# Small products of different tilings placed behind each other, and the scan's state given its own turn on VectorE and TensorE

## The chip, the cores and the metric

The kernel runs on one core of a Trainium2 chip. The metric is device time in microseconds (us) of one launch. A difference is given against the kernel before, measured on the same chip.

## The reference

One layer of a streaming encoder, sequence 256, width 4096, in fp32. A combined projection feeds 16 heads of forgetting attention (fox) and 32 heads of an RWKV-7 scan; both are gated, projected back, added to the residual and normalised.

```python
proj = jnp.einsum('bsd,dc->bsc', x, w_in)
# fox: softmax(q k^T / sqrt(128) + cumulated log forget gates) v, causal, 16 heads of 128
# rwkv: token shift, decay w, in-context rate a, normalised key kk, then per head of 64:
def frame_step(state, inp):
    r_t, w_t, k_t, v_t, a_t, b_t = inp
    sa = jnp.einsum('bhvk,bhk->bhv', state, a_t)
    state = (state * w_t[:, :, None, :] + sa[..., None] * b_t[:, :, None, :]
             + v_t[..., None] * k_t[:, :, None, :])
    return state, jnp.einsum('bhvk,bhk->bhv', state, r_t)
# group norm of y, a bonus term, then
h = jnp.concatenate([fox_out, rwkv_out], axis=-1) * jax.nn.silu(z)
x = layernorm(ALPHA * x + jnp.einsum('bsc,cd->bsd', h, w_out)) * ln_gain + ln_bias
```

## The kernel before, in words

**Large products.** Every fp32 operand of the two big projections is split into a high and a low half of a reduced format; `hi*hi`, `lo*hi` and `hi*lo` are summed in PSUM. The input projection runs over 8 head groups `n` (4 rwkv heads and 2 fox heads each) times 4 blocks `b` of 512 columns; a block takes 16 weight tiles `w{n}_{b}_{q}`, and each tile gives 12 products of 128x512, named `acc`. The output projection does the same with `wo` and `oacc`. A weight tile comes by DMA, ScalarE casts its high half (`w...h`, four buffers), VectorE subtracts for the low half (`w...l`, three buffers).

**Small products.** Between the large ones stand those of the attention and the scan. Of the scan, per head group: `gp` (pairwise products within a chunk, array tiled 64x128), `qt` and `xp` (assembling an inverse of blocks, array tiled 32x32), and then, for each of 4 chunks `c` of 64 frames:

- `rh` (`residual(c)`): state `SV` times the chunk's keys, tiled 128x64; VectorE copies it to `R`;
- `up`: inverse times `R`, on the whole array; ScalarE copies it to `UV`;
- `sp` (not in the last chunk): the state's update from `UV`, tiled 128x64; VectorE copies or adds it into `SV` of the next chunk, one half of the partitions (`j` = 0, 1) at a time; from the second chunk on it adds `sl`, the decayed state, which ScalarE makes;
- `yp`: the chunk's output from `SV` and `UV`, tiled 128x64.

So each chunk's `rh` needs the `SV` that came out of the `sp` before it. A small fp32 product appears as two instructions in the profile.

**What sets the order.** No instruction is issued when the code calls it. `Later` records every operation, and `flush` lays them out with a planner: it simulates the engines with estimated durations (`span_of`), gives each engine's free time to the ready operation with the lowest `key`, and issues in the resulting order. `main` marks the large products. Consecutive small products form one batch (`batches`) and are placed together. `mode_of` names the array's tiling: 0 for the whole array, else the tile's size; the planner charges its constant `SWITCH` (190) for a change of mode and prefers operations of the current mode while it is in a tiled one. `seen` adds the constant margin (`MARGIN`, 1000, for TensorE in the main part) to the end of what an operation waits for. Buffers are counted by `places`. Engines then run their queues in that order, and real waits are by semaphores.

Of the kernel before, what the change touches and what calls it, by code (L numbers as in the profile page):

```python
# [86 lines left out]
AHEAD = 100000  # L87
SWITCH = 190
MARGIN = 1000


MASKS = {}
# [52 lines left out]
def span_of(engine, name, args, out, ins):  # L145

    if engine == "tensor":
        n = columns(out)
        if name == "transpose":
            hold = max(2 * n / 2.4, 112)  # L150
        elif ins[-1].dtype == BF16:
            hold = 427
        elif ins[-1].dtype == F32R:
            hold = max(n * 17 / 16 / 2.4, 113)
        else:
            tile = rounded(int(ins[0].ap[0][1])), rounded(columns(ins[0]))
# [12 lines left out]
    n = max(columns(a) for a in [out, *ins])  # L169
    if engine == "vector":  # L170
        if name == "reciprocal":
            t = 130 + 6.32 * n
        elif name in ("tensor_copy", "tensor_scalar") and not any(is_psum(a) for a in [out, *ins]):
            t = 175 + n / 1.92
        else:
            t = 157 + n / 0.96 + (20 if any(is_psum(a) for a in ins) else 0)
        return max(t - 75, 60), t + 35
    if engine == "scalar":
        t = 195 + n / 1.2 + (0 if name == "copy" else 50)
        if "accum_out" in args:  # L180
# [25 lines left out]


class Op:
    __slots__ = ("engine", "call", "args", "kwargs", "hold", "lag", "after", "touches", "key", "main", "mode", "table", "parts", "bank", "ready", "start", "end")


class Later:


    def __init__(self, tc):
        self.tc, self.ops, self.count = tc, [], 0
        self.free = dict.fromkeys(ENGINES, 0.0)
        self.moved = 0.0
        self.writes, self.reads, self.banks = {}, {}, {}
        self.slots, self.left, self.main = {}, {}, False  # L220
        self.mode, self.table, self.floor, self.early = 0, 0, 0.0, set()
        self.stay = set()
        self.sooner = 0
        for e in ENGINES:
            setattr(self, e, Engine(self, e, getattr(tc.nc, e)))

    def take(self, engine, call, name, args, kwargs):
        op = Op()
        op.engine, op.call, op.args, op.kwargs = engine, call, args, kwargs
        aps = [a for a in args if hasattr(a, "tensor")]  # L230
        outs = [kwargs["out"]] if "out" in kwargs else [aps.pop(0)]
        ins = aps + [a for k, a in kwargs.items() if k not in ("out", "accum_out") and hasattr(a, "tensor")]
        if "accum_out" in kwargs:
            outs.append(kwargs["accum_out"])
        op.hold, op.lag = span_of(engine, name, kwargs, outs[0], ins)
        op.after, op.touches = set(), []
        op.main = self.main
        op.mode = mode_of(engine, name, ins)
        op.table = table_of(args, kwargs) if engine == "scalar" else 0
        op.key = self.count - self.sooner  # L240
        self.count += 1
        op.end = None
        for ap, writing in [(a, False) for a in ins] + [(a, True) for a in outs]:
            t = ap.tensor
            if not hasattr(t, "tag_meta"):
                continue
            where = t.name
            at = extent(ap)
            if where not in self.writes:
                self.writes[where], self.reads[where] = [], []  # L250
                if ap.space != bass.MemoryType.DRAM:
                    tag = t.tag
                    self.slots.setdefault(tag, [[self.floor if '_rp' in tag else 0.0] * (t.tag_meta.bufs or 1), []])[1].append(where)
                    self.left[where] = [tag, 0, 0.0, False]
            if where in self.left:
                self.left[where][1] += 1
                op.touches.append(where)
            for other, box in self.writes[where] + (self.reads[where] if writing else []):
                if box[0] < at[1] and at[0] < box[1] and box[2] & at[2] and other is not op:
                    op.after.add(other)  # L260
            (self.writes if writing else self.reads)[where].append((op, at))
        if engine == "tensor":
            bank = op.bank = outs[0].tensor.name
            if bank in self.banks:
                op.after.add(self.banks[bank])
            self.banks[bank] = op
        self.ops.append(op)

    def flush(self, stay=(), closing=None, margin=0):
# [9 lines left out]
        held = []  # L279

        def admit(op):
            op.ready = max([0.0] + [self.seen(o, op, margin) for o in op.after])
            heapq.heappush(soon[op.engine], (op.ready, op.key, id(op), op))

        for op in ops:
# [9 lines left out]
        while done < len(ops):  # L295
# [18 lines left out]
                heapq.heappush(ready[e], (op.key, id(op), op))  # L314
            _, _, op = heapq.heappop(ready[e])
            if e == "tensor" and self.mode and op.mode != self.mode:
                same = [x for x in ready[e] if x[2].mode == self.mode]
                if same:
                    heapq.heappush(ready[e], (op.key, id(op), op))
                    first = min(same)  # L320
                    ready[e].remove(first)
                    heapq.heapify(ready[e])
                    op = first[2]
            wait = self.places(op)
            if wait is None:
                held.append(op)
# [40 lines left out]
    def batches(self):  # L367

        out, last = [], None
        for op in self.ops:  # L370
            op.parts = [op]
            if op.engine == "tensor":
                if last and not op.main and op.mode == last.mode and (op.mode or op.bank == last.bank):
                    own = {id(o) for o in last.parts}
                    if not any(any(id(b) in own for b in o.after) for o in op.after if o.engine != "tensor"):
                        last.parts.append(op)
                        continue
                last = None
                if not op.main:
                    last = Op()  # L380
                    for a in ("engine", "main", "mode", "table", "key", "call", "bank"):
# [35 lines left out]
    def begin(self, op, at):  # L417
        if op.engine == "tensor" and op.mode != self.mode:
            at += SWITCH
            self.mode = op.mode  # L420
        if op.table and op.table != self.table:
            at += 1283
            self.table = op.table
# [27 lines left out]
def layer(ctx: ExitStack, tc: tile.TileContext, xt, xtok, w_lora, w_main, muv, w_o, up, par, mulora, fbias, lng, lnb, cst, out):  # L451
# [424 lines left out]
    def rwkv(n):  # L876
# [138 lines left out]
        for c in range(NCH):  # L1015
# [439 lines left out]
```

## Time and profile before

| | |
|---|---|
| median of 3 timed runs | 1947.29 us (1946.33 to 1948.76) |
| the profiled execution | 1950.54 us, its span 1948.8 us |
| granted TensorE clock | 0.998 |
| PE (TensorE) busy | 1936.5 us (99%) |
| DVE (VectorE) busy | 1370.1 us (70%) |
| ACT (ScalarE) busy | 988.2 us (51%) |
| DMA queue q1, share of 16 engines | 73.3% |

A row of the timeline gives the start, the duration, the engine, line and operation, output and inputs by the program's names, their shapes and how many were merged into the row; in square brackets stands the idle time of the engine before it and what ended it. All operations are issued from one line of the planner (L361), so groups are told apart by tile names. Numbers of buffers and head groups are left out of names there: `acc` is a large product, `w_4l` the low half of weight tile 4 of some block.

### The profile page before, as it was taken

The numbers are of one execution on the slowest core, as the hardware profiler recorded it, in microseconds if no ns is written. First come the engines' busy times: TensorE is split into PE (matmuls) and PEld (weight loads), VectorE is DVE, ScalarE is ACT, GpSimd is POOL, SyncE is SP. The second block draws the span as 40 slices with busy tenths as digits, with TensorE's granted clock in tenths as the row PEclk, the third lists the DMA queues.
The fourth block names the chain that finished last, engine by engine and source line by source line (L and its number), as shares of the span: only waits on it lengthen the run. The fifth ranks groups of instructions, "written<-read, shape, count | busy, mean of one in ns | idle before, by whom it ended". The sixth has DMA issues, their size and how long they took to land.

```text
span 1948.8 us, 28294 instructions
## 1 busy us (share of the span) xinstructions
PE 1936.5 (99%) x10153; PEld 1588.1 (81%) x10153; DVE 1370.1 (70%) x2212; ACT 988.2 (51%) x1485; POOL 75.3 (4%) x111
## 2 busy tenths in 40 slices
PE   9999999999999999999999999999999999999998
PEld 8888888878887888788878887888788878888886
DVE  6687678856885688578856885788578845765555
ACT  6554465445544654465446544654464544443332
POOL 0010001000100010001000100010001000000000
PEclk9999999999999999999999999999999999999999
DMA  9678767877787778777877787778677866866664
GB/s 335 178 207 235 221 190 199 244 201 205 202 238 201 212 200 240 201 209 200 237 200 207 202 235 200 215 200 239 192 215 207 309 201 205 285 201 199 200 194 162
DMA packets 269393, 420.14 MB, mean 216 GB/s; under 512 B 142338, under 2 KB 171028, under 8 KB 269252
## 3 DMA queue, kind: packets, MB, share of 16 engines
q1 hardware_dynamic: 268820, 417.91, 73.3%
q8 instruction: 80, 1.31, 0.3%
q14 instruction: 61, 0.50, 0.1%
q10 hardware_dynamic: 432, 0.43, 0.1%
HBM read 388.61 MB, written 29.64 MB: 215 GB/s over the span
## 4 chain that ended last, share of the span: by engine, by line
PE 98%; DMA 1%; DVE 0%; ACT 0%; DVEq 0%; issue 0%; SPq 0%
PE acc L361 73%; PE oacc L361 18%; PE accl L361 1%; PE yp L361 1%; PE gp L361 1%; PE up L361 1%; PE rh L361 1%; PE lp L361 1%; PE fsp L361 1%; PE fop L361 1%; PE sp L361 0%; PE np L361 0%; DMA h<-hd 0%; PE bkt L361 0%; PE fpt L361 0%; PE xp L361 0%
## 5 line engine op out<-in xcount | busy, mean ns | idle before, releaser
L361 PE MATMUL acc<-w_3h,x 128*128 128x512 f32 x248 | 80.3, 397 | 0.0
L361 PE MATMUL acc<-w_8h,x 128*128 128x512 f32 x248 | 79.9, 399 | 0.0
L361 PE MATMUL acc<-w_5h,x 128*128 128x512 f32 x248 | 79.7, 398 | 0.0
L361 PE MATMUL acc<-w_9h,x 128*128 128x512 f32 x248 | 79.2, 396 | 0.0
L361 PE MATMUL acc<-w_11h,x 128*128 128x512 f32 x248 | 78.9, 395 | 0.0
L361 PE MATMUL acc<-w_7h,x 128*128 128x512 f32 x248 | 78.8, 398 | 0.0
L361 PE MATMUL acc<-w_2h,x 128*128 128x512 f32 x248 | 78.5, 397 | 0.0
L361 PE MATMUL acc<-w_10h,x 128*128 128x512 f32 x248 | 78.1, 392 | 0.0
L361 PE MATMUL acc<-w_15h,x 128*128 128x512 f32 x248 | 77.9, 395 | 0.0
L361 PE MATMUL acc<-w_12h,x 128*128 128x512 f32 x248 | 77.7, 394 | 0.0
L361 DVE TENSOR_REDUCE xc<-prod 128x8 f32<-128x16 f32 (+30 forms) x248 | 73.0, 295 | 6.2
L361 PE MATMUL acc<-w_4h,x 128*128 128x512 f32 x248 | 77.2, 392 | 0.0
L361 PE MATMUL acc<-w_6h,x 128*128 128x512 f32 x248 | 77.0, 391 | 0.0
L361 PE MATMUL acc<-w_0h,x 128*128 128x512 f32 x248 | 76.7, 391 | 0.0
L361 PE MATMUL acc<-w_1h,x 128*128 128x512 f32 x248 | 76.7, 390 | 0.0
L361 PE MATMUL acc<-w_13h,x 128*128 128x512 f32 x248 | 76.5, 389 | 0.0
L361 PE MATMUL acc<-w_14h,x 128*128 128x512 f32 x248 | 76.4, 389 | 0.0
L361 DVE TENSOR_TENSOR prod<-Nb,xc 128x8 f32<-128x8 f32 (+30 forms) x248 | 71.3, 287 | 4.0 <-DMA Nb<-nd 0.4
L361 ACT CAST w_9h<-w 128x1024 fp32r<-128x1024 f32 x31 | 32.7, 1055 | 61.5 <-PE acc L361 54.4
L361 DVE TENSOR_TENSOR w_6l<-w,w_6h 128x1024 fp32r<-128x1024 f32 x31 | 38.0, 1225 | 35.0 <-PE acc L361 34.3
L361 ACT CAST w_14h<-w 128x1024 fp32r<-128x1024 f32 x31 | 32.6, 1051 | 57.9 <-PE acc L361 34.6
L361 DVE TENSOR_TENSOR w_7l<-w,w_7h 128x1024 fp32r<-128x1024 f32 x31 | 38.2, 1233 | 32.2 <-PE acc L361 16.0
(656 smaller groups left out, 5491.1 us busy)
## 6 DMA issues: line engine op xcount, KB each, us to landing
w<-in_w_main_dram SPq DMA_DIRECT2D x496, 512.0 KB, 3.9
wo<-in_w_o_dram SPq DMA_DIRECT2D x128, 512.0 KB, 3.6
bt<-bk SPq DMA_DIRECT2D x88, 128.0 KB, 4.6
Nb<-nd SPq DMA_DIRECT2D x16, 512.0 KB, 6.9
wr<-in_w_main_dram SPq DMA_DIRECT2D x15, 512.0 KB, 6.9
hd<-hl SPq DMA_DIRECT2D x29, 256.0 KB, 5.0
h<-hd SPq DMA_DIRECT2D x29, 256.0 KB, 5.7
raw<-bt SPq DMA_DIRECT2D x16, 256.0 KB, 6.8
```

Source lines behind the costliest of these rows:

```text
L361: ins = op.call(*op.args, **op.kwargs)
```

## The change

Five things, all in the planner and the scan.

- A batch may now hold products of different tilings behind each other (`batches`), as long as none of them waits for another engine's result that the batch itself feeds. Its readiness is worked out part by part (`admit`).
- Operations can be marked `urgent`: `rh` from the second chunk on, and the writes of `SV`. They get a very low `key`, and `seen` gives them a margin of 40 only.
- TensorE, in a tiled mode, may stand idle up to `PATIENCE` = 300 for an urgent batch of the same mode, and otherwise takes another tiled batch before a whole-array one.
- VectorE does not begin an operation that would still run when an urgent one comes ready.
- `rh` and the writes of `SV` are issued half by half, `j` = 1 first, in the order in which `sp` makes the halves.

```diff
@@ span_of
         elif ins[-1].dtype == BF16:
-            hold = 427
+            hold = 427 * n / 512
@@ Later.take
-        op.key = self.count - self.sooner
+        op.urgent = self.urgent
+        op.key = self.count - self.sooner - 2 * AHEAD * self.urgent
...
+        op.earliest = self.earliest
@@ flush
         def admit(op):
-            op.ready = max([0.0] + [self.seen(o, op, margin) for o in op.after])
+            op.ready, at = op.earliest, 0.0
+            for part in op.parts:
+                op.ready = max([op.ready] + [self.seen(o, op, margin) - at for o in part.after if o not in op.parts])
+                at += part.hold
...
             if e == "tensor" and self.mode and op.mode != self.mode:
-                same = [x for x in ready[e] if x[2].mode == self.mode]
-                if same:
+                soonest = [x for x in soon[e] if x[3].urgent and x[3].mode == self.mode and x[0] < at + PATIENCE]
+                same = [x for x in ready[e] if x[2].mode == self.mode] or not soonest and not op.mode and [x for x in ready[e] if x[2].mode]
+                if same or soonest:
                     heapq.heappush(ready[e], (op.key, id(op), op))
-                    first = min(same)
-                    ready[e].remove(first)
+                    first = min(same or soonest)
+                    (ready if same else soon)[e].remove(first)
...
+            elif e == "vector" and not op.urgent:
+                soonest = [x for x in soon[e] if x[3].urgent and x[0] < at + op.hold]
+                if soonest and self.places(min(soonest)[-1]) is not None:
...
@@ batches
-                if last and not op.main and op.mode == last.mode and (op.mode or op.bank == last.bank):
+                if last and not op.main and (op.mode and last.mode or op.mode == last.mode and op.bank == last.bank):
...
+                        if op.mode != last.parts[-1].mode:
+                            last.parts[-1].hold += SWITCH
@@ seen
         if op.main or op.key < 0:
-            return o.end
+            return o.end + 40 * op.urgent
@@ residual
-            for u in range(2):
-                for j in (1, 0):
+            nc.urgent = c > 0
+            for j in (1, 0):
+                for u in range(2):
                     nc.tensor.matmul(rh[HALF[j], u * C : (u + 1) * C], lt[j][:, u, c, 0:C], SV[j][:, u, c, :], start=True, stop=True)
+            nc.urgent = False
@@ rwkv, behind sp and yp
-                for j in range(2):
+                nc.urgent = True
+                for j in (1, 0):
...
                         nc.vector.tensor_tensor(SV[j][h, :, c + 1, :], so, sl[h], ALU.add)
+                nc.urgent = False
```

What it moves, on TensorE behind chunk 0 of head group 4 (`yp4` and `rh4_1` of the scan, `acc5` the large products of the next head group). Before:

```order
L361 MATMUL yp4_2446<-gb1_830,UV1_4_2317 64x64
L361 MATMUL yp4_2446<-gb0_829,UV0_4_2316 64x64
L361 MATMUL acc5_0_0_2430<-w5_0_4h_2444,x9_166 128x512 x2
L361 MATMUL acc5_0_0_2430<-w5_0_4l_2445,x9_166 128x512
L361 MATMUL acc5_0_1_2431<-w5_0_4h_2444,x9_166 128x512 x2
L361 MATMUL acc5_0_1_2431<-w5_0_4l_2445,x9_166 128x512
L361 MATMUL rh4_1_2453<-SV1_4_2315,lt1_4_2233 64x64
L361 MATMUL rh4_1_2453<-SV0_4_2314,lt0_4_2232 64x64
```

Now, at the same place:

```order
L379 MATMUL yp4_2446<-gb1_830,UV1_4_2317 64x64
L379 MATMUL yp4_2446<-gb0_829,UV0_4_2316 64x64
L379 MATMUL rh4_1_2453<-SV1_4_2315,lt1_4_2233 64x64 x2
L379 MATMUL rh4_1_2453<-SV0_4_2314,lt0_4_2232 64x64 x2
L379 MATMUL acc5_0_1_2431<-w5_0_4l_2445,x9_166 128x512
```

The six large products between `yp4` and `rh4_1` are gone from there, and the halves of `rh` no longer alternate.

On TensorE around `xp4`, where `rh4_0` stood alone, 13 large products ahead of `xp4`. Before:

```order
L361 MATMUL acc5_0_0_2430<-w5_0_3h_2438,x6_159 128x512
L361 MATMUL xp4_2440<-X_828,Q4_2436 32x32 x16
L361 MATMUL acc5_0_0_2430<-w5_0_3h_2438,x6_159 128x512
L361 MATMUL acc5_0_0_2430<-w5_0_3l_2439,x6_159 128x512
L361 MATMUL acc5_0_1_2431<-w5_0_3h_2438,x6_159 128x512 x2
```

Now:

```order
L379 MATMUL acc5_0_0_2430<-w5_0_3l_2439,x6_159 128x512
L379 MATMUL xp4_2440<-X_828,Q4_2436 32x32 x16
L379 MATMUL rh4_0_2441<-SV1_4_2315,lt1_4_2233 64x64 x2
L379 MATMUL rh4_0_2441<-SV0_4_2314,lt0_4_2232 64x64 x2
L379 MATMUL acc5_0_1_2431<-w5_0_3h_2438,x6_159 128x512 x2
```

`rh4_0` has moved behind `xp4`, a 128x64 tiling straight behind a 32x32 one.

On VectorE behind `sp4_0`, with what each row waits for. Before:

```order
L361 TENSOR_TENSOR w5_0_6l_2458<-w5_0_6_2443,w5_0_6h_2457 128x1024 [waits DMAHW3_49,DVE_49,PE_49]
L361 COPY SV1_4_2315<-sp4_0_2448 64x2x64 [waits PE_49]
L361 COPY SV0_4_2314<-sp4_0_2448 64x2x64
L361 TENSOR_TENSOR w5_0_7l_2465<-w5_0_7_2450,w5_0_7h_2464 128x1024 [waits DVE_49,DMAHW7_49,PE_49,Activation_49]
L361 COPY R4_1_2454<-rh4_1_2453 128x128 [waits PE_49]
```

Now:

```order
L379 TENSOR_TENSOR w5_0_6l_2458<-w5_0_6_2443,w5_0_6h_2457 128x1024 [waits DMAHW3_49,DVE_49,PE_49]
L379 COPY SV1_4_2315<-sp4_0_2448 64x2x64 [waits PE_49]
L379 COPY SV0_4_2314<-sp4_0_2448 64x2x64
L379 COPY R4_1_2454<-rh4_1_2453 128x128 [waits PE_49]
L379 TENSOR_TENSOR w5_0_7l_2465<-w5_0_7_2450,w5_0_7h_2464 128x1024 [waits DVE_49,DMAHW7_49,PE_49,Activation_49]
```

The weight subtraction between the state and `R` has moved behind `R`; in both, one wait stands ahead of the two copies of the state.

More of the change, by code (lines that the diff above doesn't have):

```diff
@@ L89 @@
 MARGIN = 1000
+PATIENCE = 300
 MASKS = {}
@@ L208 @@
 class Op:
-    __slots__ = ("engine", "call", "args", "kwargs", "hold", "lag", "after", "touches", "key", "main", "mode", "table", "parts", "bank", "ready", "start", "end")
+    __slots__ = ("engine", "call", "args", "kwargs", "hold", "lag", "after", "touches", "key", "main", "mode", "table", "parts", "bank", "urgent", "earliest", "ready", "start", "end")
 class Later:
@@ L222, in __init__ @@
         self.stay = set()
-        self.sooner = 0
+        self.sooner, self.urgent, self.earliest = 0, False, 0.0
         for e in ENGINES:
@@ L316, in flush @@
             if e == "tensor" and self.mode and op.mode != self.mode:
-                same = [x for x in ready[e] if x[2].mode == self.mode]
-                if same:
+                soonest = [x for x in soon[e] if x[3].urgent and x[3].mode == self.mode and x[0] < at + PATIENCE]
+                same = [x for x in ready[e] if x[2].mode == self.mode] or not soonest and not op.mode and [x for x in ready[e] if x[2].mode]
+                if same or soonest:
                     heapq.heappush(ready[e], (op.key, id(op), op))
-                    first = min(same)
-                    ready[e].remove(first)
+                    first = min(same or soonest)
+                    (ready if same else soon)[e].remove(first)
                     heapq.heapify(ready[e])
-                    op = first[2]
+                    heapq.heapify(soon[e])
+                    op = first[-1]
+                    at = max(at, op.ready)
+            elif e == "vector" and not op.urgent:
+                soonest = [x for x in soon[e] if x[3].urgent and x[0] < at + op.hold]
+                if soonest and self.places(min(soonest)[-1]) is not None:
+                    heapq.heappush(ready[e], (op.key, id(op), op))
+                    first = min(soonest)
+                    soon[e].remove(first)
+                    heapq.heapify(soon[e])
+                    op = first[-1]
+                    at = max(at, op.ready)
             wait = self.places(op)
@@ L380, in batches @@
                     last = Op()
-                    for a in ("engine", "main", "mode", "table", "key", "call", "bank"):
+                    for a in ("engine", "main", "mode", "table", "key", "call", "bank", "urgent", "earliest"):
                         setattr(last, a, getattr(op, a))
@@ L419, in begin @@
             at += SWITCH
-            self.mode = op.mode
+        if op.engine == "tensor":
+            self.mode = op.parts[-1].mode
         if op.table and op.table != self.table:
```

## The prediction

> **What bounds the kernel now.** I read the page first: the busy shares and the chain that ended last.
>
> ```profile
> span 1948.8 us, 28294 instructions
> PE 1936.5 (99%) x10153; PEld 1588.1 (81%) x10153; DVE 1370.1 (70%) x2212; ACT 988.2 (51%) x1485; POOL 75.3 (4%) x111
> PE 98%; DMA 1%; DVE 0%; ACT 0%; DVEq 0%; issue 0%; SPq 0%
> ```
>
> TensorE (PE) is the bound from end to end, and nothing else holds more than 1% of the chain. So a change here is worth what it takes out of, or puts into, PE's stream, and VectorE's (DVE's) time counts only where PE waits for it. The list of the chain's pieces gives the price of the large products when nothing lies between them:
>
> ```profile
> 1613.66 313.75 PE oacc L361 x1384
> ```
>
> 313.75 / 1384 = 0.2267 us from one large product to the next. Everything below is measured against this pitch: I take a stretch between two large products, subtract 0.2267 for each large product in it, and what is left is the price of the small products between them, switches included. I read that from PE's timeline at the scan of head group 4:
>
> ```profile
> 1000.68 0.40 PE L361 MATMUL acc<-w_4l,x 128*128 128x512 f32 x1
> 1001.00 0.46 PE L361 MATMUL sp<-UV,BKt 128*64 128x64 f32 x8
> ...
> 1001.64 0.29 PE L361 MATMUL yp<-gb,UV 128*64 128x64 f32 x4
> 1001.86 0.73 PE L361 MATMUL acc<-w_4h,x 128*128 128x512 f32 x2
> 1002.43 0.40 PE L361 MATMUL acc<-w_4l,x 128*128 128x512 f32 x1
> ...
> 1003.12 0.40 PE L361 MATMUL acc<-w_4l,x 128*128 128x512 f32 x1
> 1003.45 0.45 PE L361 MATMUL rh<-SV,lt 128*64 128x64 f32 x8
> 1003.83 0.73 PE L361 MATMUL acc<-w_5h,x 128*128 128x512 f32 x2
> 1004.40 0.40 PE L361 MATMUL acc<-w_5l,x 128*128 128x512 f32 x1
> ```
>
> A view of each tile's instructions gives one small product's own duration (least, median, most, in ns):
>
> ```profile
> L361 PE MATMUL sp<-UV,BKt x192: 222/222/270, 241.2 to 1600.4; 128*64 128x64 f32 x192
> L361 PE MATMUL xp<-X,Q x256: 191/191/212, 234.7 to 1581.0; 32*32 32x32 f32 x128
> ```
>
> sp with yp costs 1002.43 - 1000.68 - 3 x 0.2267 = 1.07 us; rh alone costs 1004.40 - 1003.12 - 0.68 = 0.60. Of the 1.07, the products themselves (first sp start to last yp start: 1001.00 to 1001.64, plus 0.29 - 0.22 within that last group of four) are 0.71, call it 0.70. The other 0.37 is the visit's fixed price: the first small product starts 0.32 behind the large one instead of 0.23, and the second large product after it starts about 0.34 behind the first. For rh, 0.60 - 0.37 leaves 0.23 of products. A visit that is joined to another saves at most these 0.37, and that is the whole gain the change can have.
>
> **The change part by part.** The order of the changed kernel has three kinds of places in the scan. Sixteen times rh stands directly behind sp and yp (chunks 0 and 2 in head groups 1 to 6; chunks 0 and 1 in 0 and 7). Eight times rh of chunk 0 stands directly behind xp. Eight times rh still stands alone, one to three large products behind yp. So 24 visits fewer; at 0.37 each that is 8.9 us, if nothing were paid for it.
>
> *The sixteen behind yp.* rh reads the state SV that DVE makes from sp. What DVE takes for it, when it is free:
>
> ```profile
> 1001.52 0.61 DVE L361 COPY SV<-sp 64x128 f32<-64x128 f32 x2 [0.57 <-PE sp L361]
> 248.99 0.61 DVE L361 TENSOR_TENSOR SV<-sp,sl 64x128 f32<-64x128 f32 x2 [1.73 <-PE sp L361]
> 248.40 0.46 PE L361 MATMUL sp<-UV,BKt 128*64 128x64 f32 x8
> ```
>
> Chunk 0 copies: sp starts at 1001.00, the first half's copy at +0.52, both halves are done at +1.13. Later chunks add sl: from 248.40, start +0.59, done +1.20. The last sp product starts at about +0.24 and runs about 0.22, so +0.52 is 0.06 behind the end of the whole sp. In the built order the first state copy carries the wait for PE and the second none, so the first half does not start when its own products are done but after all of sp. Issuing the halves in the order in which sp makes them therefore brings the first half no earlier. yp's last product starts at +0.70. PE comes free for rh then, and has to wait for the state; sixteen small products of yp don't cover the DVE pair. How fast PE follows DVE, a wait of the profile shows:
>
> ```profile
> 1072.51 0.61 PE L361 MATMUL acc<-w_11h,x 128*128 128x512 f32 x2
> 1073.98 0.73 PE L361 MATMUL np<-shl,onesr 128*128 128x512 f32 x2 [0.86 <-DVE shl L361]
> 1073.24 0.68 DVE L361 TENSOR_TENSOR shl<-sb,shl 128x512 fp32r<-128x512 f32 x1
> ```
>
> DVE ends at 1073.92, PE starts at 1073.98: 0.06. All large products queue behind such a wait. So rh's second half begins at +1.13 + 0.06 = +1.19, and its four products spread over 0.12 (half of sp's 0.24): last start +1.31. The joined visit costs 0.37 + 1.31 = 1.68 in chunk 0 and 0.37 + 1.38 = 1.75 with sl, against 1.07 + 0.60 = 1.67 for the two apart. Eight times +0.01 and eight times +0.08: 0.7 us **lost**. What the switch gives, the wait takes back. The bounds: no wait at all would make it 0.37 + 0.70 + 0.24 = 1.31, a gain of 0.36 each, 5.8 us; DVE held up by its weight subtraction would make it a loss of 0.79 each (rivals).
>
> *The eight behind xp.* Here no DVE result is awaited, as SV of chunk 0 is long there. The price of xp:
>
> ```profile
> 995.50 0.39 PE L361 MATMUL acc<-w_3h,x 128*128 128x512 f32 x1
> 995.81 0.69 PE L361 MATMUL xp<-X,Q 32*32 32x32 f32 x32
> 996.44 0.50 PE L361 MATMUL acc<-w_3h,x 128*128 128x512 f32 x1
> 996.77 0.40 PE L361 MATMUL acc<-w_3l,x 128*128 128x512 f32 x1
> 997.01 0.39 PE L361 MATMUL acc<-w_3h,x 128*128 128x512 f32 x1
> ```
>
> 997.01 - 995.50 - 0.68 = 0.83, of which 0.50 is products (0.69 less the last one's 0.19) and 0.33 fixed. Joined: fixed 0.35 (half of each kind), 0.50 xp, 0.23 rh, and J, the step from a 32x32 tiling straight to a 128x64 one: 1.08 + J against 0.83 + 0.60 = 1.43. The trace has no such step. Its nearest rows: xp to a large product is 996.44 - 996.31 = 0.13, and full-array transposes straight into sp are
>
> ```profile
> 1599.72 0.49 PE L361 MATMUL fpt<-cs,lg 128*128 128x128 f32 x3
> 1600.14 0.46 PE L361 MATMUL sp<-UV,BKt 128*64 128x64 f32 x8
> ```
>
> 0.20 from the third transpose (1599.94, at 0.11 a piece) to sp. J lies between 0.02 (the step within xp) and 0.35 (nothing saved); I take 0.15, between the two rows. Gain 0.20 x 8 = 1.6 us, bounds 2.6 and 0.
>
> The Trainium skill (TensorEngine Tiling (Array Packing), Key Properties) says that changing the tiling mode, and not just the tile, drains TensorE. By that rule a small product placed behind one of another tiling still pays a drain. With last xp product's 0.19 and a late start of 0.09 as at 1001.00, J would be 0.28, the gain 0.07 x 8 = 0.6, and the sum at the end of this part +0.3 instead of -0.7. The step of 0.20 above speaks for some drain, not for all of that.
>
> *The eight that stand alone.* Where three large products lie between the last low-half product of a weight tile and sp, DVE is in the next subtraction when sp comes:
>
> ```profile
> 1009.67 0.39 PE L361 MATMUL acc<-w_6l,x 128*128 128x512 f32 x1
> 1009.99 0.46 PE L361 MATMUL sp<-UV,BKt 128*64 128x64 f32 x8
> 1010.16 1.23 DVE L361 TENSOR_TENSOR w_9l<-w,w_9h 128x1024 fp32r<-128x1024 f32 x1 [1.25 <-issue]
> 1011.30 0.58 DVE L361 TENSOR_TENSOR SV<-sp,sl 64x128 f32<-64x128 f32 x2
> ```
>
> The subtraction holds DVE from 0.49 until 1.63 behind the low-half product. With three large products between, sp starts 4 x 0.23 + 0.09 = 1.0 behind it, so the state begins at +0.63 and is done at about +1.24. rh behind two large products starts at +0.70 + 0.15 + 0.34 + 0.32 = +1.5. No wait, no gain: 0.
>
> *The rest.* rh's products in the new order of halves spread like sp's, 0.24 against 0.23: 16 x 0.01 = 0.2 us lost in the visits that don't wait. DVE held free before a state costs its weight subtractions up to 1.2 us now and then; a low half is used two weight tiles after its buffer came free, 24 x 0.23 = 5.4 us, so PE does not see it. The scan closes 24 large products earlier in most groups; its followers still stand where block boundaries put them, and PE had no idle time there to win. qt, gp, up, bkt and the fox products keep their visits.
>
> Sum: -1.6 + 0.7 + 0.2 = **-0.7 us**. The profiled execution took 1950.54 (span 1948.8), above the median of the timed runs, 1947.29. It holds some waits that need not recur, such as the 0.86 at np above. I put the sum on the median: **1946.6 us**. A difference under about 0.2%, 3.9 us, I call no change that can be told here.
>
> **The rivals.**
> *Faster: the state comes in time (0.16).* If the first half's copy starts when its own products are done, 0.12 earlier, or DVE's pair overlaps more closely, the sixteen joined visits gain up to 0.36 each: 1946.6 - 0.7 - 5.8 = 1940.1 at the full price. For it: DVE had nothing else to do for 0.57 us before 1001.52. Against it: the copy starts 0.06 behind the end of the whole sp, and the two halves need 0.61 however they are ordered, with only 0.46 of yp left beside them.
>
> *Slower: a weight subtraction gets in front of the state (0.14).* In each of the sixteen visits the row ahead of SV on DVE is a weight subtraction, and PE now waits with it. At 1009.99 the state began at +1.31 instead of +0.52; that is 0.79 more of PE standing, 12.6 us if it befell all sixteen: 1959.2. Before, four to nine large products between yp and rh covered it. The point: the state wants DVE 0.52 after sp starts, so the subtraction's 1.63 are over in time if four or more large products stand between the low-half product and sp (5 x 0.23 + 0.09 + 0.52 = 1.76). The new order has eleven in most of the sixteen and never under five. Against the rival, then, unless weight transfers come late and push the subtraction back by over 1.6 us; five such events would already cost 3.9.
>
> *The joining buys nothing (0.12).* J is a full drain and refill, 0.35: the eight gain nothing, the sum is +0.9, 1948.2. This ends within 0.2% as well.
>
> **How the numbers follow.** My own case (0.58) and the last rival give no change that can be told. The faster rival at half its price is -3.6, so most but not all of it counts as faster; the slower one counts from five events. Faster 0.15, same 0.72, slower 0.13. Range: my case from J's ends is 1945.6 to 1948.2; the timed runs before scatter from 1946.33 to 1948.76, which adds about 1.4 up and 1 down; half the price of the faster rival and four late events of the slower one carry it to 1943.0 and 1950.2.
>
> **What would show it.** In the profile after, rh behind yp should start its first half 0.87 after sp and its last product at about +1.31 (+1.38 in later chunks), PE idle until SV, and the two large products around such a visit should lie 1.68 to 1.75 further apart than their pitch. rh behind xp should begin about 0.15 after xp's last product, and the joined visit cost 1.23. I am wrong if rh behind yp starts without waiting (faster), or if SV starts later than +0.6 there (slower), or if other tiles, qt or np, hold PE for microseconds that they didn't hold before.

## The result, and the profile after

The changed kernel takes 1951.16 us (median of 22 runs, 1949.86 to 1957.16), the kernel before 1948.71 (22 runs, 1946.33 to 1951.3): ratio 1.0014, 95% interval 1.0008 to 1.002, so 2.5 us slower. The forecast was 1946.6, no change that can be told, and its range ended at 1950.2. With 22 runs the kernel before stands 1.4 us above the median of three on which the forecast was put; the change itself was forecast at -0.7 and is +2.5.

The page's span, busy shares and chain:

```profile
span 1950.2 us, 28283 instructions
PE 1935.2 (99%) x10153; PEld 1591.9 (82%) x10153; DVE 1375.6 (71%) x2212; ACT 988.6 (51%) x1485; POOL 72.2 (4%) x111
PE 98%; DMA 1%; DVE 1%; issue 0%; ACT 0%; ACTq 0%; DVEq 0%; SPq 0%
```

PE is still the bound, with the same number of matmuls. DVE now holds 1% of the chain, where it held 0%.

The timeline at chunk 0 of head group 4, where `rh` now stands behind `sp` and `yp`:

```profile
1003.96 0.61 PE L379 MATMUL acc<-w_4h,x 128*128 128x512 f32 x2
1004.51 0.46 PE L379 MATMUL sp<-UV,BKt 128*64 128x64 f32 x8
...
1005.02 0.61 DVE L379 COPY SV<-sp 64x128 f32<-64x128 f32 x2 [1.71 <-PE sp L379]
1005.14 0.29 PE L379 MATMUL yp<-gb,UV 128*64 128x64 f32 x4
1005.37 0.76 PE L379 MATMUL rh<-SV,lt 128*64 128x64 f32 x8
1006.06 0.50 PE L379 MATMUL acc<-w_4l,x 128*128 128x512 f32 x1
...
1006.40 0.63 PE L379 MATMUL acc<-w_5h,x 128*128 128x512 f32 x2
```

The state's copies begin 0.51 behind `sp`, `rh` begins 0.86 behind it. The visit costs 1006.40 - 1003.96 - 3 x 0.2267 = 1.76 us, where 1.68 was forecast and 1.67 was read there for the two apart. In chunk 2 the state is a sum and starts later:

```profile
1016.31 0.40 PE L379 MATMUL acc<-w_7l,x 128*128 128x512 f32 x1
1016.64 0.46 PE L379 MATMUL sp<-UV,BKt 128*64 128x64 f32 x8
...
1017.23 0.61 DVE L379 TENSOR_TENSOR SV<-sp,sl 64x128 f32<-64x128 f32 x2 [1.78 <-PE sp L379]
...
1017.57 0.76 PE L379 MATMUL rh<-SV,lt 128*64 128x64 f32 x8
1018.26 0.73 PE L379 MATMUL acc<-w_7h,x 128*128 128x512 f32 x2
...
1018.83 0.40 PE L379 MATMUL acc<-w_7l,x 128*128 128x512 f32 x1
```

1018.83 - 1016.31 - 3 x 0.2267 = 1.84. Taken in this way at the trace's full resolution, eight visits cost 1.75 to 1.76 and eight 1.82 to 1.84, all sixteen 28.7 us together. In the kernel before, `sp` with `yp` cost 1.06 on average and a lone `rh` 0.585, so sixteen of both apart are 16 x 1.645 = 26.3 (the forecast took 1.67 from one of each). The joining behind `yp` loses **2.4** us, not 0.7.

Behind `xp`:

```profile
997.92 0.39 PE L379 MATMUL acc<-w_3l,x 128*128 128x512 f32 x1
998.24 0.69 PE L379 MATMUL xp<-X,Q 32*32 32x32 f32 x32
998.87 0.46 PE L379 MATMUL rh<-SV,lt 128*64 128x64 f32 x8
999.25 0.73 PE L379 MATMUL acc<-w_3h,x 128*128 128x512 f32 x2
999.82 0.40 PE L379 MATMUL acc<-w_3l,x 128*128 128x512 f32 x1
```

The joined visit costs 999.82 - 997.92 - 3 x 0.2267 = 1.22 (1.21 to 1.22 in all eight at the trace's full resolution). That is the forecast 1.23, a gain of **1.6** us.

These two leave +0.8. Most of the rest is in a row of PE's waits, here before and after:

```profile
PE np L361 <- DVE shl L361: 0.9, 1, 0.9
```

```profile
PE np L379 <- DVE shl L379: 4.0, 4, 1.8
```

After, PE waits for `np` four times, 4.0 us in all (the columns are total, times, longest). `np` belongs to the preparation of the next group's heads; in the built order it has moved with the scan: 12 large products earlier in the even heads from head 4 on, 41 later in head 2 (and 21 later in head 3). What it waits for, at head 8 (ACT is ScalarE):

```profile
871.44 1.05 ACT L379 CAST w_10h<-w 128x1024 fp32r<-128x1024 f32 x1 [1.87 <-DMA w<-in_w_main_dram]
872.40 0.91 ACT L379 ACTIVATE s<-raw,omm 128x256 f32<-128x256 f32 x2
872.94 0.88 DVE L379 SCALAR_TENSOR_TENSOR s<-raw,prm,s 128x255 f32<-128x255 f32 x2 [1.91 <-ACT s L379]
...
877.22 1.23 DVE L379 TENSOR_TENSOR w_11l<-w,w_11h 128x1024 fp32r<-128x1024 f32 x1
878.36 0.69 DVE L379 TENSOR_TENSOR shl<-sb,shl 128x512 fp32r<-128x512 f32 x1
879.10 0.73 PE L379 MATMUL np<-shl,onesr 128*128 128x512 f32 x2 [0.77 <-DVE shl L379]
```

And before, at the same head:

```profile
871.01 1.06 ACT L361 CAST w_11h<-w 128x1024 fp32r<-128x1024 f32 x1 [1.35 <-DMA w<-in_w_main_dram]
871.97 0.91 ACT L361 ACTIVATE s<-raw,omm 128x256 f32<-128x256 f32 x2
...
877.92 0.69 DVE L361 TENSOR_TENSOR shl<-sb,shl 128x512 fp32r<-128x512 f32 x1
879.35 0.62 PE L361 MATMUL np<-shl,onesr 128*128 128x512 f32 x2
```

The chain from `s` to the end of `shl` takes 6.65 us in both. It begins when ACT has cast the weight tile that stands ahead of it, and that cast waits for its transfer. After, it stands behind tile 10 instead of tile 11, but tile 10 comes no sooner on the clock. PE's place for `np` has moved 12 x 0.23 = 2.7 us ahead, which uses up the 0.7 us that lay between `shl` and `np` before. The wait is only 0.77, because PE's row as a whole stood 1.5 us later on the clock by then and the chain 0.4.

The two profiles themselves differ by 1.4 us of span. Sorted by what stands between the large products, `np` takes 3.8 us more after than before and the other small products 0.9; `qt` takes 1.05 less (PE's wait for a transfer there was 1.1 before and 0.4 after), and large products that follow each other directly take 2.0 less. The profiled execution before held waits of its own: at 1950.54 it took 1.8 more than the median of its 22 runs.

### The profile page after: what moved, and what is told of

It is laid out like the page before. It is cut to its first block, busy times and chain, and to the rows that moved or that the text cites. A ratio compares the mean times of both kernels' runs of the same rounds, so it can differ in the third digit from the quotient of the medians.

```text
span 1950.2 us, 28283 instructions
## 1 busy us (share of the span) xinstructions
PE 1935.2 (99%) x10153; PEld 1591.9 (82%) x10153; DVE 1375.6 (71%) x2212; ACT 988.6 (51%) x1485; POOL 72.2 (4%) x111
## 4 chain that ended last, share of the span: by engine, by line
PE 98%; DMA 1%; DVE 1%; issue 0%; ACT 0%; ACTq 0%; DVEq 0%; SPq 0%
PE acc L379 72%; PE oacc L379 18%; PE accl L379 1%; PE rh L379 1%; PE yp L379 1%; PE gp L379 1%; PE up L379 1%; PE lp L379 1%; PE fsp L379 1%; PE fop L379 1%; PE sp L379 0%; PE np L379 0%; DMA h<-hd 0%; PE bkt L379 0%; PE fpt L379 0%; PE xp L379 0%
## 5 line engine op out<-in xcount | busy, mean ns | idle before, releaser
L379 ACT CAST w_8h<-w 128x1024 fp32r<-128x1024 f32 x31 | 32.6, 1050 | 47.9 <-PE acc L379 40.4
```

The costliest lines, as they stand in the source:

```text
L379: ins = op.call(*op.args, **op.kwargs)
```

## The experiments

All kernels were timed in five rounds against the kernel before. Theory A is the price of the visits: the joined ones are dear because PE stands until the state is written. What else costs was open at first, and split later into N (the new places of `np`) and S (waits of that one execution). B and C are told in the expectations that name them. The 5.1 and 5.06 us that two expectations give for `np` in the first profile are 4.0 in its row.

**Nothing urgent.** `xp` and `rh` still join; `rh` of the later chunks goes back behind large products, and `np` goes back to its old places of itself.

```diff
-            nc.urgent = c > 0
+            nc.urgent = False
...
-                nc.urgent = True
+                nc.urgent = False
```

> The changed kernel with nothing marked urgent: rh still stands directly behind xp (8 joined visits), but behind yp it stands alone again, four to five large products later, and np of the even heads is back where it stood before the change. Theory A (the loss is the waiting of rh behind yp, 2.2 us, plus np placed ahead of its data; the join with xp is a gain of 1.6): the joined xp visit costs 1.23 us, rh alone 0.60, np waits like those of before, total 1.6 us faster than before, ratio 0.9992. Theory B (np's waits in the profile of the changed kernel are accidents of one execution, the loss is in the visits alone): the same, 0.9992. Theory C (the join's gain is given back elsewhere, for instance by the halves of rh no longer alternating): 1.000.

1947.76 us, ratio 0.9994 (0.9985 to 1.0003). The view of waits has no row for `np`. The sixteen joined visits gone, the time is about 1 us below the kernel before, near `xp`'s 1.6, though the interval also holds no change. The gain of `xp` is shown by the rows of its visits, not by the time.

**np of the even heads six steps later instead of four** (all joined visits kept, one more joined).

```diff
-        yield from wait(W["np"] if n else 2 * W["np"])
+        yield from wait((6 if u == 0 else W["np"]) if n else 2 * W["np"])
```

> The changed kernel with two slots more of waiting ahead of np of the even heads, which puts it back to where it stood before the change (12 large products later); 17 visits sp, yp, rh stay joined, 8 visits xp, rh too; qt and the scan come some 20 large products later. Theory A: np's waits go (5.1 us of idle PE in the profile of the changed kernel, about 1.2 before), the joined visits still cost 1.77 and 1.85, total +2.3 - 1.6 = 0.7 us over before, ratio 1.0004. Theory B: as slow as the changed kernel, 1.0014.

1950.64, ratio 1.0006 (0.9997 to 1.0015); `np` waits 1.6 us in all. The even heads from head 4 on stand where they stood before, the odd ones 12 later; head 2 still stands 42 later and still waits 1.17. The visits stay at 1.76 to 1.83. The ratio is near theory A's 1.0004, but the interval holds the kernel before and, barely, theory B's 1.0014 too.

**rh from an older state**, meant to free `rh` of VectorE; `rh` is changed by it.

```diff
-    ... lt[j][:, u, c, 0:C], SV[j][:, u, c, :], ...
+    ... lt[j][:, u, c, 0:C], SV[j][:, u, max(c - 1, 0), :], ...
```

> The changed kernel, but rh of the second and later chunks reads the state of one chunk earlier, which is long there, so that it waits for no VectorE result; the output is another one for that. Sixteen visits sp, yp, rh are joined as in the changed kernel, np stands where the changed kernel has it. Theory A: such a visit costs 0.37 + 0.71 + 0.24 = 1.32 us instead of 1.77 and 1.85, 7.9 us less over sixteen, np's waits stay (2 to 4 us): total about 1944, ratio 0.997 to 0.998 to before. Theory B: no lasting np waits, 0.9963. If the wait for the state is not what makes the joined visits dear, the visit stays near 1.8 and the ratio at 1.0014.

1952.41, ratio 1.0017 (1.0008 to 1.0025). A miss of design: the planner then joined `rh` of chunk c + 2 behind `sp` of chunk c, which writes the very state it reads. Sixteen visits stayed at 1.76 to 1.84, and seven lone `rh` waited too (1.05 instead of 0.60). It says nothing on a visit without the wait.

**Only np early, in the kernel before** (even heads from head 4 on 14 large products earlier, odd heads from head 3 on 24, no visit joined).

```diff
-        yield from wait(W["np"] if n else 2 * W["np"])
+        yield from wait((0 if u == 0 else W["np"]) if n else 2 * W["np"])
```

> The kernel before with nothing changed but the waiting ahead of np of the even heads: no slots instead of four, which puts np of the even heads 14 large products earlier (the changed kernel has it 12 earlier) and what follows it, qt and the scan, up to 24 earlier. Theory A: PE stands idle at np of the even heads until VectorE has the shl tile, 3 to 6 us in all, ratio 1.0015 to 1.003. Theory B: no more than in the kernel before, ratio 1.000.

1948.94, ratio 1.0001 (0.9992 to 1.001), with 1.7 us of waits at `np`. That spoke against the 3 to 6 us of theory A; a cost of up to 1.9 us lies within the interval. Head 2 had not moved in this kernel, however, and `rh`, `xp` and the rest of the scan had moved too.

**rh that waits for nothing from VectorE**: from chunk 1 on it reads `UV` of the chunk before (its result is changed by that).

```diff
-            nc.urgent = c > 0
+            nc.urgent = False
...
-    ... SV[j][:, u, c, :], start=True, stop=True)
+    ... (UV[j][:, u, c - 1, :] if c else SV[j][:, u, c, :]), start=True, stop=True)
```

> The changed kernel with the state taken out of rh's way: from chunk 1 on rh multiplies UV of the chunk before instead of the state SV, so it waits for nothing that VectorE makes from sp (this part of the computation is changed). The order then joins all 24 rh of chunks 1 to 3 behind sp and yp; head and np stand as in the changed kernel. Theory A (the joined visits are dear because PE stands until VectorE has copied the state, and a visit without that wait costs 0.37 fixed + 0.71 for sp and yp + 0.24 for rh = 1.32 us): sixteen visits cost 1.32 instead of 1.77 to 1.85, 7.8 us less, and eight more are joined for 1.32 instead of 1.06 + 0.61 = 1.67, 2.8 us less; together 10.6 below the changed kernel, about 1940.5, ratio to the kernel before 0.9958. Rival C (small products of different tiles behind each other are dear by themselves: the switch between banks or tiles, not VectorE): the visits stay at 1.7 or more and the ratio at 1.000 or above.

1941.57, ratio 0.9956 (0.9944 to 0.9969), against 0.9958 by theory A. PE's timeline at the place shown above:

```profile
996.35 0.61 PE L379 MATMUL acc<-w_4h,x 128*128 128x512 f32 x2
996.90 0.46 PE L379 MATMUL sp<-UV,BKt 128*64 128x64 f32 x8
...
997.53 0.29 PE L379 MATMUL yp<-gb,UV 128*64 128x64 f32 x4
997.64 0.45 PE L379 MATMUL rh<-UV,lt 128*64 128x64 f32 x8
998.02 0.50 PE L379 MATMUL acc<-w_4l,x 128*128 128x512 f32 x1
998.36 0.62 PE L379 MATMUL acc<-w_5h,x 128*128 128x512 f32 x2
```

`rh` starts 0.11 behind the last group of `yp`, the pitch within `yp`. The visit costs 998.36 - 996.35 - 0.68 = 1.33, and all 24 cost 1.33 to 1.34; the forecast's bound without a wait was 1.31. So the joining is worth what was said, and VectorE's state takes it back. The rival (the switch itself is dear) is out. In this execution `np` of the even heads from head 4 on stands 12 earlier, as in the changed kernel, and waits 0.4 us in all; it was the fastest of its five runs (1938.85). So these places alone don't fix how long PE waits there.

**The halves of rh alternating again**, every visit where the changed kernel has it.

```diff
-            for j in (1, 0):
-                for u in range(2):
+            for u in range(2):
+                for j in (1, 0):
```

> The changed kernel with rh's four products alternating between the two halves again, as before the change; every visit stands where it stands in the changed kernel. Theory A (the two halves are two column tiles that run side by side, so that one half alone takes 0.22 and both take 0.23; both wait for the second half's state at +1.18): the sixteen visits stay at 1.77 and 1.85 within 0.04, and the lone rh too; ratio as the changed kernel's, 1.0014. By the premise of the forecast (a half takes half the time) alternating would put 0.12 more behind the second half's state and cost 0.12 in each of sixteen, 1.9 us, ratio 1.0024. It is also a second profile with the places of np of the changed kernel. Theory N (np of even heads stands too early in the changed kernel and waits for VectorE in every execution): idle of PE in front of np sums to 3 us or more again. Theory S (the waits of 5.06 us at np were that one execution's): under 2.

1951.25, ratio 1.0013 (1.0004 to 1.0022), visits 1.75 to 1.84, as theory A had it:

```profile
1004.36 0.61 PE L379 MATMUL acc<-w_4h,x 128*128 128x512 f32 x2
1004.90 0.46 PE L379 MATMUL sp<-UV,BKt 128*64 128x64 f32 x8
...
1005.77 0.76 PE L379 MATMUL rh<-SV,lt 128*64 128x64 f32 x8
...
1006.79 0.63 PE L379 MATMUL acc<-w_5h,x 128*128 128x512 f32 x2
```

1006.79 - 1004.36 - 0.68 = 1.75. Issuing one half ahead of the other buys nothing. Why, the two halves of `rh` in the changed kernel's visit show, each cut out of its timeline by a window:

```profile
1005.37 0.45 PE L379 MATMUL rh<-SV,lt 128*64 128x64 f32 x4
```

```profile
1005.69 0.45 PE L379 MATMUL rh<-SV,lt 128*64 128x64 f32 x4
```

Four instructions of one half (two products, as an fp32 product is two instructions) take 0.45 us; all eight of both take 0.46 where nothing is awaited (at 998.87 above). The halves are two column tiles of the array that run side by side, whatever the order of issue: 998.87 is issued half by half, and `rh` of the kernel before, which alternates, takes the same 0.45 (at 1003.45 in the prediction). Only a wait between them sets them one behind the other. In either order the last half starts with the second half of the state and then takes its own 0.45. The `np` waits came back in this execution, with `np` at the changed kernel's places: 3.8 us.

```profile
PE np L379 <- DVE shl L379: 3.8, 3, 1.5
```

**The changed kernel once more.**

> The changed kernel unchanged, profiled once more, in the same rounds as the three others. Theory N (np of even heads stands too early, so PE waits for it in every execution): PE stands 3 us or more in front of np again, at the same heads, and the time is 2 to 3 us above the kernel before. Theory S (these waits were that execution's own): under 2 us at np; then the time above the price of the visits must come from scattered waits for weights, and the kernel's time is 0.5 to 1.5 us above the kernel before. Ratio 1.0014 by N, 1.0003 to 1.0008 by S.

1952.72, ratio 1.0016 (1.0007 to 1.0025), and at `np` 1.8 us:

```profile
PE np L379 <- DVE shl L379: 1.8, 3, 0.9
```

The size is S's (under 2) and the time is N's; the execution with 1.8 was the fastest of its eleven (1950.07). In all three profiles with these places (the first, this one, and the one with the halves alternating) PE waits at the same three heads: 2 (1.75, 0.94, 1.30 us), 8 (0.77, 0.50, 1.46) and 10 (1.16, 0.39, 1.03). So these waits are not one execution's own; what sets their length isn't shown. Over all profiles: where heads 8 and 10 stand 9 to 14 large products earlier than in the kernel before, PE waits 0.5 to 2.5 us at the two together, in all eight profiles; where they stand at their old places or later, it waits in one of six (0.86).

**np moved without the joined visits**, in the kernel with nothing urgent, beside that kernel in the same rounds. Head 2 stands 42 later than before the change, the even heads from head 6 on stand 14 earlier. Other than expected, head 4 and the odd heads from head 5 on stand 24 earlier and head 3 stands 42 later, which the changed kernel does not have.

```diff
-        yield from wait(W["np"] if n else 2 * W["np"])
+        yield from wait(((11 if n == 1 else 0) if u == 0 else W["np"]) if n else 2 * W["np"])
```

> The kernel of the first experiment (nothing urgent, rh behind xp joined, the sixteen rh behind yp apart as before the change), with np of the even heads set where the whole change puts it: head 2 by 42 large products later, heads 4 to 14 by 14 earlier than in the kernel before. The visits of the scan stay as they are. Theory N (np at these places waits for VectorE, whatever the visits of the scan cost): PE stands 1 us or more in front of np of head 2, 0.5 or more at heads 8 and 10, 2.3 to 4.7 us in all as in the three profiles with np at these places, and the time is 1 to 3 us above the same kernel without the shift. Theory S (the waits belong to the joined visits, or cost nothing in the end as weights are late anyway): under 1 us at np, or the time within 0.6 us of the same kernel without the shift.

> The kernel of the first experiment once more, in the same rounds as the one with np shifted, so that the two are compared on one chip. By all theories as before: visits 1.6 us below the kernel before, np waits under 0.5 us, ratio 0.9992 to 0.9996.

Shifted 1952.09, ratio 1.0019 (1.001 to 1.0027); not shifted 1947.92, ratio 0.9997 (0.9988 to 1.0006). Nothing but the waiting ahead of `np` differs, and 4.2 us go; the intervals lie apart. Waits of PE, shifted, then not shifted:

```profile
PE np L379 <- DVE shl L379: 2.7, 3, 1.2
PE up L379 <- DVE R L379: 1.4, 1, 1.4
```

```profile
PE np L379 <- DVE shl L379: 0.6, 1, 0.6
```

Theory N had 2.3 to 4.7 us at `np`, which came, and 1 to 3 in the time, which was more, with a new wait at `up` in it. The 2.1 more at `np` and the 1.4 at `up` make 3.5 of the 3.8 us by which the two spans differ, so here the waits cost about what they last. It missed one place: head 2, 42 later, didn't wait here, and head 4 did (1.24), at a place 24 earlier; heads 8 and 10 waited 0.67 and 0.78. So the places of the preparation are worth some us though the scan's visits cost the same, but this order is not the changed kernel's, and its 4.2 us are not the size of that kernel's term. The kernel not shifted came a little off its expectation too: 0.6 us at `np` where under 0.5 was said, and 0.9997 where 0.9996 was the end.

**A version that makes the state sooner.** Only chunk 1's `rh` is joined; the halves of `sp` of chunk 0 lie in two PSUM banks, one copied by VectorE, one by ScalarE, which is held free for it in the same way.

```diff
-            elif e == "vector" and not op.urgent:
+            elif e in ("vector", "scalar") and not op.urgent:
...
-            nc.urgent = c > 0
+            nc.urgent = c == 1
...
+                sps = (pst(f"sp{n}_{c}_0") if c == 0 else sp, sp)
...
-                        nc.vector.tensor_copy(SV[j][h, :, 1, :], so)
+                        (nc.vector.tensor_copy if j else nc.scalar.copy)(SV[j][h, :, 1, :], so)
```

> The changed kernel with the state made sooner: only rh of chunk 1 is placed behind sp and yp (eight visits), the two halves of sp of chunk 0 lie in two PSUM banks, and the half j=1 is copied to SV by VectorE and the half j=0 by ScalarE at the same time; ScalarE is held free for its copy as VectorE is; the other rh stand apart. Theory A (what a joined visit costs is the time until both halves of the state are there): both copies begin at +0.52 and are done by about +0.9 to +1.0, rh's last product starts at +1.13 to +1.2, and the visit costs 1.50 to 1.57 against 1.67 apart, 0.8 to 1.4 us less for eight; with xp and rh joined (1.6 less) about 2.4 to 3 us below the kernel before, ratio 0.9985 to 0.9988. Rival C (the visit's price is switches and banks): two banks of sp make it 1.8 or more, and the ratio is 1.000 or above. If ScalarE's copy is held up by a cast in front of it, it starts later than +0.7 and the visit costs over 1.7.

1947.11, ratio 0.9991 (0.9982 to 1.0). The timeline:

```profile
1001.93 0.61 PE L379 MATMUL acc<-w_4h,x 128*128 128x512 f32 x2
1002.48 0.46 PE L379 MATMUL sp<-UV,BKt 128*64 128x64 f32 x8
...
1002.96 0.29 DVE L379 COPY SV<-sp 64x128 f32<-64x128 f32 x1 [1.68 <-PE sp L379]
...
1003.02 0.26 ACT L379 COPY SV<-sp 64x128 f32<-64x128 f32 x1 [1.86 <-PE sp L379]
...
1003.31 0.47 PE L379 MATMUL rh<-SV,lt 128*64 128x64 f32 x8
...
1004.04 0.63 PE L379 MATMUL acc<-w_5h,x 128*128 128x512 f32 x2
```

The two copies lie side by side, the state is there 0.80 behind `sp` instead of 1.12, and the visit costs 1004.04 - 1001.93 - 0.68 = 1.43 against 1.645 apart, better than expected. The eight gain 1.7 us; with `xp` that should be 3.3, and 1.6 were measured, less than the 2.4 to 3 expected; 3.3 still lies within the interval. `np` waits 1.1 here. Each half of `rh` follows its own copy: the first starts at 1003.31, 0.06 behind the end of VectorE's, and the second, cut out by a window that begins as the first half's first instruction ends (its other three are still in the row), 0.05 behind the end of ScalarE's:

```profile
1003.33 0.45 PE L379 MATMUL rh<-SV,lt 128*64 128x64 f32 x7
```

**That version with np of the even heads set back**, from head 6 on to the old places and, in the second kernel, to 12 behind them (head 4 stays 9 and 8 ahead, the odd heads from head 5 on go 6 and 12 behind).

```diff
-        yield from wait(W["np"] if n else 2 * W["np"])
+        yield from wait((5 if u == 0 and n > 1 else W["np"]) if n else 2 * W["np"])
```

> The kernel with the state in two banks and copied by two engines, and besides np of the even heads from head 4 on set back to the places it had before the change (nine large products later). Theory N (the change's second cost is PE waiting for np, because np stands nearer to a chain of small operations that on ScalarE lies behind the cast of a weight tile that came late; where np stands further back, the wait is gone): PE's idle in front of np falls from 1.7 us to 1.0 or less, as in the kernel before; joined visits stay at 1.44; time 3 to 3.5 below the kernel before, ratio 0.9982 to 0.9985. Theory S (these waits move to another place in PE's row when np is moved: the late weights set the pace there anyway): np waits less, but the time stays at 0.9988 to 0.9995.

The other has 6 for the 5.

> The same with np of the even heads from head 4 on set 21 large products later (12 later than in the kernel before); the scan of each of these groups then stands about 20 later too. Theory N: no idle in front of np from head 4 on (at most 0.3 us), time 3.3 to 4 us below the kernel before, ratio 0.9980 to 0.9983. Theory S: no idle at np, but the time stays at 0.9988 or above, and the idle shows at large products that wait for weight casts, or at qt.

1945.98, ratio 0.9987 (0.9978 to 0.9996), and 1945.76, ratio 0.9986 (0.9977 to 0.9995). Both intervals lie below the kernel before, by 0.1% in the middle, and below the changed kernel's. Against the same version with `np` unmoved (0.9991) they gain less than the intervals can tell, and they stand between N's numbers and S's: inconclusive on that. The second also waited 0.46 at head 6, where theory N allowed 0.3 at most.

## Why the prediction was wrong

**The step that failed first** is the spread of `rh`'s second half: "its four products spread over 0.12 (half of sp's 0.24)". Its begin was right: the state written at 1005.02 + 0.61 = 1005.63, PE behind that by the 0.06 of the `np` row, 1.18 after `sp` (1.19 forecast). But one half takes as long as both, 0.22 from the first start to the last, because the halves run side by side. So the last product of a joined visit starts at +1.40 instead of +1.31, and 16 x 0.09 = 1.5 of the 1.7 us between the forecast +0.7 and the measured +2.4 are this step. The rest is in the price list: the pair apart cost 1.645 and not 1.67 (+0.4), the fixed price was 0.36 and not 0.37 (-0.2). The Trainium skill (TensorEngine Tiling (Array Packing), Key Properties) says that tiles work independently and can run matmuls in parallel; the 0.45 for one half and 0.46 for both agree.

The same holds for `sp`, whose eight also take 0.46: its halves end together, so there was no first half that could have been copied 0.12 earlier, as the faster rival supposed, and the order in which the change issues the halves has nothing to gain.

**The second step** is the rest, put at 0: PE "had no idle time there to win". That `np` moves with the scan was not priced, and its slack (0.7 us at head 8) was not looked up. The 0.86 at `np`, set aside as a wait that "need not recur", indeed did not recur at its head 10 in the four other profiles with that head at its old place. But the rows show 4.0, 1.8 and 3.8 us at `np` with the changed kernel's places, mean 3.2; with the old places (before, and nothing urgent twice) 0.9, none and 0.6, mean 0.5: **+2.7**. Visits and `np` make -1.6 + 2.4 + 2.7 = +3.5, against 2.5 in the time, whose interval is 1.6 to 3.9. So the direction and the two terms are shown, and the size of the second is known to a microsecond or two only. Why head 2 waits when it stands 41 or 42 later stays open: it waited with the joined visits (0.94 to 1.75) and not without them. The forecast named this as what would make it wrong ("other tiles, qt or np").

Of the 4.6 us between 1946.6 and 1951.16, 1.4 are not the change: the median of three on which the sum was put lay that much below the median of 22.

**What held.** The price list, to 0.03: fixed 0.37, a visit without waits 1.31 (measured 1.33). The step J from the 32x32 tiling to 128x64: the last `xp` product starts at 998.24 + 0.69 - 0.19 = 998.74, `rh` at 998.87, so 0.13 (0.15 forecast). The 0.28 that the prediction worked out under the rule of a drain in the Trainium skill (TensorEngine Tiling (Array Packing), Key Properties) did not come; the switch is paid, 0.13 against 0.02 within `xp`, but it is cheap. The faster rival did not come: the copies start 0.51 and 0.59 behind `sp`, whichever half goes first. The slower one did not either: in none of the sixteen did the state begin later than +0.6, so a weight subtraction was never in front of it. In the built order the rule that holds VectorE free changes nothing: without it the same order comes out on PE, DVE, ACT and SP (no run was made of that).

## What to carry to other kernels

Joining two visits of small products saves the whole fixed price of one (0.37 us here) only if the second needs nothing that another engine makes from the first; otherwise count the other engine's whole turn, start, halves and wake-up, against it. Where two engines cut that turn by 0.32 us, joining paid (1.43 against 1.645). Where two column tiles run side by side, the products of one take as long as those of both. When a change moves a stage, list what else moves with it in the order and give each a slack from the trace before: `np` had 0.7 us at head 8 and was moved by 2.7. A wait that one profile shows may be that execution's own and still tell that the slack there is small; a second profile of the same order tells which waits belong to the order.

## What the runs showed of the hardware that was not expected

- Four instructions on one 64-column half of the array take 0.45 us, eight on both halves 0.46 when issued half by half and 0.45 when alternating (128x64 tiling, fp32, two instructions to a product).
- From a 32x32 tiling straight to a 128x64 one it takes 0.13 us from the last start to the next, as from `xp` to a large product before.
- VectorE and ScalarE, copying from two PSUM banks at the same time (0.29 and 0.26 us), brought the whole state 0.32 us sooner than VectorE's pair, and each half of `rh` began 0.05 to 0.06 behind the end of its own copy.
